# Table preload, operand splits and transposes around a seven-product SwiGLU

## The chip, the core and the metric

The kernel runs on one NeuronCore of a Trainium2 chip. The metric is the device time of one execution in microseconds, and the lower it is the better. A core has a matrix engine (PE, which loads a stationary operand of 128x128 and streams a moving one past it), a vector engine (DVE), a scalar engine (ACT, which evaluates functions from tables that have to be loaded), a general engine (POOL) and a queue engine (SP) from which most transfers are issued. Each engine takes its own instructions in order, and they wait for each other through semaphores. SBUF is the on-chip memory, PSUM the eight banks into which the PE accumulates.

## The reference

One residual encoder layer for a sequence of 512 tokens (with 16 learned tokens in front), model width D = 1024 and feed-forward width 2816:

```
xn = rmsnorm(h); proj = xn @ w_in          # both attentions' q, k, v
o_sb = stick-breaking attention            # 8 heads of 128
o_df = differential attention              # 8 heads, 2 maps each
gates = sigmoid(xn @ w_gate + b_gate)
h = h + (gates0 * (o_sb @ w_br_sb) + gates1 * (o_df @ w_br_df)) @ w_out
hn = rmsnorm(h)
h = h + (silu(hn @ w_ffn_gate) * (hn @ w_ffn_up)) @ w_ffn_down
out = rmsnorm(h)[16:]
```

All inputs are float32. The change touches the last three lines: the second norm, the SwiGLU and the final norm.

## The kernel before

**Precision.** Each float32 operand is split into a high part in the PE's fp32r type and a low part, the remainder: `split` has ACT copy the high part (L74, a CAST) and DVE subtract it (L75). A product is then three matmuls (`mm3`: L159 high x high, L160 and L161 high x low). Weights come as chunks of 512 KB, issued on SP's queue into `wst` (three buffers; `wsu`, two, for the up projection's), and are split to `wh` and `wl` (four buffers each).

**The stages that matter here.** The output projection (`accumulate(..., "out", ...)`) makes its left 512 columns in the four z accumulators and its right 512 in the four mm accumulators, and finishes the right half token tile by token tile: add to `hres` (L819), square with a running sum (L822), then `rstd`: Ln (L238) and Exp (L240) on ACT and a Newton step on DVE (L249, L245, L247), then the normed tile `hn` (L847). `turned(0)` and `turned(1)` transpose `hn` of tokens 0 to 255 and 256 to 511 on the PE into PSUM and take from it `hT_h` (ACT), `hT_l` (DVE) and a plain float32 copy `bf` (ACT, L863).

**The SwiGLU** runs over 22 column blocks f of 128 features. Block 0 is done plainly (`early`, in two token halves). The blocks 1 to 21 use a scheme that makes a 2x2 block product from seven products instead of eight: the token side is cut by token half and by half of the model width, and combined once into t1, t2, t3, t4 (`block_sums`, L868 to L876, each split into a high and a low part); the weight side of each block is combined into s2 and s1 (`c2`), s3 (`c3`) and s4 (`c4`). A block is `first` (a11 x b11 and a12 x b21, the weights of `c1`), `second` (s2 x t2, s1 x t1, s3 x t3) and `third` (a22 x t4, s4 x b22), 12 matmuls each. Between them ACT copies partial sums out of PSUM (qx, qy, L992 and L997), because the next product goes on in the same accumulator, and DVE adds them. The SiLU of the two token halves is L985 and L1009; the result is `aT`.

**The down projection** then streams `w_ffn_down` against splits of `aT` called `da` (eight buffers, made in `act`), left half in z, right half in mm, and ends tile by tile as above, with the final scaling on DVE (L1053) and ACT (L1055) and the stores on SP (L1054, L1056).

**What sets the order.** The tile framework's scheduler orders each engine's instructions from the program's order and priorities; evacuations of PSUM are lifted by `tc.high_priority`. `use_table` loads an ACT function set and keeps it in program order relative to other such pins, while ordinary activations may be placed on either side of it; where a function's set is not the loaded one, a load is put right ahead of it:

```
def use_table(name):
    tc.keep_in_program_order(nc.scalar.preload_act_table_set(name))
```

Buffers come from rings, so an instruction that writes one waits for the last reader of its former content.

Of the kernel before, what the change touches and what calls it, by code (L numbers as in the profile page):

```python
# [39 lines left out]
def block_kernel(ctx: ExitStack, tc: tile.TileContext, x, meta, norm_mix_g, w_in, w_gate, b_gate,  # L40
# [808 lines left out]
    def turned(tp_):  # L849
        cs = slice(tp_ * 256, (tp_ + 1) * 256)  # L850
        for k in range(0, KT, 2):
            pt = tr_tile()
            for i in range(2):
                for t in range(2):
                    nc.tensor.transpose(pt[:, (2 * i + t) * P:(2 * i + t + 1) * P],
                                        hn[:, 2 * tp_ + t, (k + i) * P:(k + i + 1) * P], ident)
            for i in range(2):
                g = g_ffn[:, k + i:k + i + 1]
                p = pt[:, i * 256:(i + 1) * 256]
                nc.scalar.activation(hT_h[:, k + i, cs], p, AF.Copy, scale=g)  # L860
                nc.vector.scalar_tensor_tensor(hT_l[:, k + i, cs], p, g, hT_h[:, k + i, cs].bitcast(F32),  # L861
                                               op0=ALU.mult, op1=ALU.subtract)
                nc.scalar.activation(bf[k // 4][tp_][:, (k + i) % 4], p, AF.Copy, scale=g)  # L863

    def block_sums():
        (b11, b12), (b21, b22) = bf
        sub, add = ALU.subtract, ALU.add
        nc.vector.tensor_tensor(b11, b11, b12, op=sub)  # L868
        nc.vector.tensor_tensor(b12, b22, b12, op=sub)
        nc.vector.tensor_tensor(b22, b11, b22, op=add)  # L870
        nc.vector.tensor_tensor(b21, b22, b21, op=sub)
        th, tl = tsum["t2"]
        nc.scalar.activation(th, b22, AF.Copy, scale=-1.0)
        nc.vector.scalar_tensor_tensor(tl, b22, -1.0, th.bitcast(F32), op0=ALU.mult, op1=sub)
        for n, v in (("t1", b11), ("t3", b12), ("t4", b21)):
            split(*tsum[n], v)  # L876
# [26 lines left out]


    with tc.tile_pool(name="ffn", bufs=1) as fp:
        aT = fp.tile([P, NFF, SEQ], F32, name="aT")
        gF = fp.tile([P, D], F32, name="gF")
        nc.gpsimd.dma_start(gF, norm_final_g.rearrange("(o d) -> o d", o=1).broadcast_to([P, D]))
        ffw_ctx = ExitStack()
        fw = ffw_ctx.enter_context(tc.tile_pool(name="ffw", bufs=1))  # L910
        fpools["w"] = fw
        ops = {}

        def chunk(n):
            return tuple(wpool.tile([P, KT, P], F32R, tag=t, name=t) for t in ("wh", "wl"))

        def c1(f):
            wh, wl = chunk(1)
            split(wh, wl, staged[at_of["fg", f]])
            ops[f, "a11"], ops[f, "a12"] = (wh[:, K1], wl[:, K1]), (wh[:, K2], wl[:, K2])  # L920

        def c2(f):
# [3 lines left out]
            nc.vector.tensor_tensor(s[:, K1], s[:, K2], g[:, K1], op=ALU.add)  # L926
            wh, wl = chunk(2)
            split(wh, wl, s)
# [3 lines left out]
        def c3(f):  # L932
            g, u = staged[at_of["fg", f]], staged[at_of["fu", f]]
            nc.vector.tensor_tensor(u[:, K1], g[:, K1], u[:, K1], op=ALU.add)
            wh, wl = chunk(3)
            split(wh, wl, u)
            ops[f, "s3"], ops[f, "a22"] = (wh[:, K1], wl[:, K1]), (wh[:, K2], wl[:, K2])

        def c4(f):
            g, s = staged[at_of["fg", f]], ops[f, "s"]  # L940
            nc.vector.tensor_tensor(g[:, K2], s[:, K1], g[:, K2], op=ALU.add)
            wh, wl = chunk(4)
# [22 lines left out]

        bank = {}

        def product(f, w, t, ps, start, stop):
            (wh, wl), (th, tl) = ops[f, w], tsum[t]
            mm3(ps, [(wh[:, k], wl[:, k], th[:, k], tl[:, k]) for k in range(4)], start, stop, True)  # L970

        def quarter(name, bufs=2):
            return fw.tile([P, 256], F32, tag=name, bufs=bufs, name=name)

        def first(f):
            e1, e2, e3 = mm_tile()[:, 0:256], mm_tile()[:, 0:256], z_tile()[:, 0, 0:256]
            sg = fw.tile([P, SEQ], F32, tag="sg", bufs=2, name="sg")
            bank[f] = e1, e2, e3, sg
            product(f, "a11", "b11", e1, True, True)
            product(f, "a12", "b21", e2, True, True)  # L980
            with tc.high_priority(offset=EVAC):
# [5 lines left out]
        def second(f):  # L987
            e1, e2, e3, sg = bank[f]
            qx, qy = quarter("qx"), quarter("qy")
            product(f, "s2", "t2", e1, False, True)  # L990
            with tc.high_priority(offset=EVAC):
                nc.scalar.copy(qx, e1)  # L992
            ready(at_job(c3, f) + 2)
            product(f, "s1", "t1", e3, True, True)
            product(f, "s3", "t3", e1, False, True)
            with tc.high_priority(offset=EVAC):
# [4 lines left out]
        def third(f, qx, qy):  # L1001
            e1, e2, e3, sg = bank[f]
            product(f, "a22", "t4", e1, False, True)
            with tc.high_priority(offset=EVAC):
                nc.vector.scalar_tensor_tensor(aT[:, f, T1], e1, -1.0, sg[:, T1], op0=ALU.mult, op1=ALU.mult)
            product(f, "s4", "b22", e3, False, True)
            with tc.high_priority(offset=EVAC):
# [22 lines left out]
        dw_ctx = ExitStack()  # L1030
        dw = dw_ctx.enter_context(tc.tile_pool(name="dw", bufs=1, reuse_waits="tile"))
        acts = []

        def act(half, k):
            m = half * NFF + k
            for i in range(len(acts), min(2 * NFF, m + 3)):
                a = dw.tile([P, 2, SEQ], F32R, tag="da", bufs=8, name="da")
                split(a[:, 0], a[:, 1], aT[:, i % NFF])
                acts.append(a)
            return acts[m][:, 0], acts[m][:, 1]  # L1040

# [57 lines left out]
```

## Time and profile before

| what | us |
|---|---|
| median of the runs (1008.54 to 1009.72, 3 runs) | 1009.62 |
| profiled execution, its own time | 1009.99 |
| its span, first to last instruction | 1008.2 |
| PE busy | 974.9 |
| PEld (weight loads, beside PE) | 880.4 |
| DVE busy | 659.9 |
| ACT busy | 544.7 |
| POOL busy | 109.7 |

The profile is one execution on the chip. Its page gives each engine's busy time, the groups of instructions by line with what ended the idle time ahead of them, and the chain that ended last; the trace behind it can be asked for waits, for windows of time, and for single instructions in order of time. In a row of an instruction stand its start, its duration, the engine, the line, the operation, output and input tile, and in brackets the idle time before it and what ended that. Matmuls are pipelined, so the distance between starts says more than a duration. The SwiGLU and the down projection take the span from 631.7 us to the end.

### The profile page before, as it was taken

The numbers are of one execution on the slowest core, as the hardware profiler recorded it, in microseconds if no ns is written. First come the engines' busy times: TensorE is split into PE (matmuls) and PEld (weight loads), VectorE is DVE, ScalarE is ACT, GpSimd is POOL, SyncE is SP. The second block draws the span as 40 slices with busy tenths as digits, with TensorE's granted clock in tenths as the row PEclk, the third lists the DMA queues.
The fourth block names the chain that finished last, engine by engine and source line by source line (L and its number), as shares of the span: only waits on it lengthen the run. The fifth ranks groups of instructions, "written<-read, shape, count | busy, mean of one in ns | idle before, by whom it ended". The sixth has DMA issues, their size and how long they took to land. (4 is left out here: it accounts for less than half of the span.)

```text
span 1008.2 us, 16022 instructions
## 1 busy us (share of the span) xinstructions
PE 974.9 (97%) x6285; PEld 880.4 (87%) x6285; DVE 659.9 (65%) x1214; ACT 544.7 (54%) x1026; POOL 109.7 (11%) x152
## 2 busy tenths in 40 slices
PE   7999999999999999999999999899999999899993
PEld 5999899998989999889878888899999999788883
DVE  7665446667777777777663335988888887645532
ACT  5655564555465666565643334764555555644436
POOL 4000000000022222122022320000000000000002
PEclk9999999999999999999999999999999999999997
DMA  6322222222333332333223252243333342322202
GB/s 197 105 64 63 84 85 63 85 64 71 93 90 87 104 99 72 83 85 96 74 83 105 93 178 64 63 128 104 112 99 115 95 118 71 123 87 105 88 17 84
DMA packets 129743, 93.13 MB, mean 92 GB/s; under 512 B 3682, under 2 KB 114435, under 8 KB 129667
## 3 DMA queue, kind: packets, MB, share of 16 engines
q1 hardware_dynamic: 127506, 85.09, 27.8%
q0 software_dynamic: 2000, 6.95, 2.7%
q8 instruction: 49, 0.80, 0.3%
q14 instruction: 28, 0.22, 0.1%
q10 hardware_dynamic: 160, 0.07, 0.0%
HBM read 85.67 MB, written 2.10 MB: 87 GB/s over the span
## 5 line engine op out<-in xcount | busy, mean ns | idle before, releaser
L75 DVE TENSOR_TENSOR wl<-wst,wh 128x1024 fp32r<-128x1024 f32 (+1 forms) x150 | 174.3, 1162 | 150.2 <-ACT wh L74 149.8
L159 PE MATMUL mm<-xT_h,wh 128*128 128x264 f32 (+2 forms) x776 | 249.9, 322 | 1.0 <-DVE dk L427 0.8
L160 PE MATMUL mm<-xT_l,wh 128*128 128x264 f32 (+2 forms) x776 | 247.2, 319 | 1.6 <-DVE xT_l L633 1.6
L161 PE MATMUL mm<-xT_h,wl 128*128 128x264 f32 (+2 forms) x776 | 246.8, 318 | 0.0
L74 ACT CAST wh<-wst 128x1024 fp32r<-128x1024 f32 (+1 forms) x150 | 148.6, 992 | 172.4 <-PE mm L160 112.0
L159 PEld LDWEIGHTS mm<-xT_h,wh 128*128 128x128 f32 x776 | 146.9, 189 | 11.3 <-PE tr L315 1.0
L160 PEld LDWEIGHTS mm<-xT_l,wh 128*128 128x128 f32 x776 | 146.8, 189 | 10.8 <-DVE xT_l L633 1.8
L161 PEld LDWEIGHTS mm<-xT_h,wl 128*128 128x128 f32 x776 | 146.7, 189 | 10.0
L159 PE MATMUL mm<-hT_h,wh 128*128 128x256 f32 x284 | 80.6, 286 | 1.8 <-ACT hT_h L860 0.9
L160 PE MATMUL mm<-hT_l,wh 128*128 128x256 f32 x284 | 81.1, 286 | 1.0 <-DVE hT_l L861 1.0
L161 PE MATMUL mm<-hT_h,wl 128*128 128x256 f32 x284 | 81.0, 286 | 0.2 <-DVE wl L75 0.2
L159 PEld LDWEIGHTS mm<-hT_h,wh 128*128 128x128 f32 x284 | 53.9, 191 | 2.7 <-ACT hT_h L860 1.4
L160 PEld LDWEIGHTS mm<-hT_l,wh 128*128 128x128 f32 x284 | 54.3, 191 | 1.5 <-DVE hT_l L861 1.4
L161 PEld LDWEIGHTS mm<-hT_h,wl 128*128 128x128 f32 x284 | 54.3, 191 | 0.4 <-DVE wl L75 0.4
L159 PE MATMUL mm<-o_h,wh 128*128 128x512 f32 x128 | 53.2, 415 | 0.0
L160 PE MATMUL mm<-o_l,wh 128*128 128x512 f32 x128 | 50.1, 391 | 0.8 <-DVE o_l L518 0.8
L161 PE MATMUL mm<-o_h,wl 128*128 128x512 f32 x128 | 50.1, 391 | 0.0
L159 PE MATMUL mm<-t_h,wh 128*128 128x256 f32 x168 | 47.4, 282 | 0.5 <-ACT qy L997 0.5
L160 PE MATMUL mm<-t_l,wh 128*128 128x256 f32 x168 | 47.2, 281 | 0.0
L161 PE MATMUL mm<-t_h,wl 128*128 128x256 f32 x168 | 47.2, 282 | 0.0
L159 PE MATMUL z<-wh,da 128*128 128x512 f32 (+1 forms) x110 | 41.3, 376 | 4.0 <-ACT da L74 4.0
L296 POOL COPY v_s<-vT 128x16 f32<-128x16 f32 x64 | 21.8, 369 | 210.0 <-ACT vT L301 210.0
(278 smaller groups left out, 2236.3 us busy)
## 6 DMA issues: line engine op xcount, KB each, us to landing
wst<-in_w_in_dram SPq DMA_DIRECT2D x46, 512.0 KB, 3.9
wst<-in_w_ffn_gate_dram SPq DMA_DIRECT2D x22, 512.0 KB, 3.8
wst<-in_w_ffn_down_dram SPq DMA_DIRECT2D x22, 512.0 KB, 3.5
wsu<-in_w_ffn_up_dram SPq DMA_DIRECT2D x21, 512.0 KB, 3.7
wst<-in_w_gate_dram SPq DMA_DIRECT2D x16, 512.0 KB, 4.1
dk<-dk POOLq DMA_DIRECT2D x16, 264.0 KB, 5.0
wst<-in_w_br_sb_dram SPq DMA_DIRECT2D x8, 512.0 KB, 3.5
wst<-in_w_br_df_dram SPq DMA_DIRECT2D x8, 512.0 KB, 3.5
```

The lines of the kernel that those rows point to most:

```text
L74: (hi_copy or nc.scalar.copy)(hi, src)
L75: (lo_eng or nc.vector).tensor_tensor(lo, src, hi.bitcast(F32), op=ALU.subtract)
L159: nc.tensor.matmul(ps, lhsT=ah, rhs=bh, start=(start and i == 0), stop=False, skip_group_check=skip)
L160: nc.tensor.matmul(ps, lhsT=ah, rhs=bl, start=False, stop=False, skip_group_check=skip)
L161: nc.tensor.matmul(ps, lhsT=al, rhs=bh, start=False, stop=(stop and i == n - 1), skip_group_check=skip)
L296: nc.gpsimd.tensor_copy(v_s[:, 32 * t:32 * t + NM], vT[:, (t + 1) * P:(t + 1) * P + NM])
```

## The change

Eight edits, all behind the output projection:

1. `turned` writes its transposes into z accumulators instead of the mm ring, and makes the `bf` copies in a loop of their own behind the hT parts.
2. `block_sums` splits t1 as soon as its sum is made, and t2 ahead of the sum for t4.
3. `c1(1)` and `first(1)` (the products of block 1) move ahead of the second token half of block 0; `first` keeps the matmuls, and the evacuation becomes `first_out`.
4. The job list therefore starts with `c1(2)`.
5. The first three splits of `aT` are made inside the last block, ahead of its `third` (`act_parts(3)`).
6. The eight `da` buffers are four in the SwiGLU's freed `wsu` and `s21` buffers and four in a new pool.
7. `use_table(LN_EXP)` moves from behind the block loop into the last block, right behind `third` with its last SiLU.
8. The pools of the SwiGLU stay open to the end.

```diff
     def turned(tp_):
         cs = slice(tp_ * 256, (tp_ + 1) * 256)
+        banks = [z_tile() for _ in range(2)]
         for k in range(0, KT, 2):
-            pt = tr_tile()
+            pt = banks[k // 4][:, k // 2 % 2]
...
-                nc.scalar.activation(bf[k // 4][tp_][:, (k + i) % 4], p, AF.Copy, scale=g)
+        for k in range(KT):
+            nc.scalar.activation(bf[k // 4][tp_][:, k % 4], banks[k // 4][:, k // 2 % 2, k % 2 * 256:(k % 2 + 1) * 256],
+                                 AF.Copy, scale=g_ffn[:, k:k + 1])
 
     def block_sums():
...
         nc.vector.tensor_tensor(b11, b11, b12, op=sub)
+        split(*tsum["t1"], b11)
         nc.vector.tensor_tensor(b12, b22, b12, op=sub)
         nc.vector.tensor_tensor(b22, b11, b22, op=add)
-        nc.vector.tensor_tensor(b21, b22, b21, op=sub)
         th, tl = tsum["t2"]
         nc.scalar.activation(th, b22, AF.Copy, scale=-1.0)
         nc.vector.scalar_tensor_tensor(tl, b22, -1.0, th.bitcast(F32), op0=ALU.mult, op1=sub)
-        for n, v in (("t1", b11), ("t3", b12), ("t4", b21)):
+        nc.vector.tensor_tensor(b21, b22, b21, op=sub)
+        for n, v in (("t3", b12), ("t4", b21)):
             split(*tsum[n], v)
...
+    def first(f):
+        bank[f] = [mm_tile()[:, 0:256], mm_tile()[:, 0:256]]
+        product(f, "a11", "b11", bank[f][0], True)
+        product(f, "a12", "b21", bank[f][1], True)
+
+    c1(1)
     turned(1)
+    first(1)
     for ps, key in zip(early, (("fg", 0), ("fu", 0))):
         proj(ps[:, 256:512], weights(key), hT, slice(256, 512))
     block_sums()
...
-        jobs = [(c1, 1), (c1, 2), (c2, 1), (c3, 1), (c4, 1)]
+        jobs = [(c1, 2), (c2, 1), (c3, 1), (c4, 1)]
...
+        dw, acts = None, []
+
+        def act_parts(upto):
+            for i in range(len(acts), min(2 * NFF, upto)):
+                pool, tag, bufs = ((dw, "da", 4), (fw, ("wsu", "s21")[i % 2], 2))[i % 8 < 4]
+                a = pool.tile([P, 2, SEQ], F32R, tag=tag, bufs=bufs, name="da")
+                split(a[:, 0], a[:, 1], aT[:, i % NFF])
+                acts.append(a)
...
         for f in range(1, NFF):
...
+            if f == NFF - 1:
+                act_parts(3)
             third(f, *rest)
+            if f == NFF - 1:
+                use_table(LN_EXP)
             ready(at_job(c4, f) + 2)
-        use_table(LN_EXP)
-        ffw_ctx.close()
         tp_ctx.close()
```

**Where instructions now stand.** On ACT at the end of the last token tiles (L822 squares, L238 Ln, L240 Exp, L1055 and L1071 the scaled output), before:

```order
L822 ACTIVATE sq,ssq<-hres 128x256
L1055 ACTIVATE outs<-outs,rs 128x512
L822 ACTIVATE sq,ssq<-hres 128x256
L238 ACT_TABLE_LOAD
L238 ACTIVATE rs<-ssq 128x1
L240 ACT_TABLE_LOAD
L240 ACTIVATE rs<-rs 128x1
L1055 ACTIVATE outs<-outs,rs 128x512
```

and now:

```order
L822 ACTIVATE sq,ssq<-hres 128x256
L1071 ACTIVATE outs<-outs,rs 128x512
L822 ACTIVATE sq,ssq<-hres 128x256
L238 ACTIVATE rs<-ssq 128x1
L240 ACTIVATE rs<-rs 128x1
L1071 ACTIVATE outs<-outs,rs 128x512
```

The two loads are gone from each of the four tiles, eight in all.

On ACT at the end of the last SwiGLU block (sg the SiLU, qx and qy the copies out of PSUM, wh the down projection's weights, da the splits of aT), before:

```order
L1009 ACTIVATE sg<-sg 128x256
L66 ACT_TABLE_LOAD
L992 COPY qx<-mm 128x256
L74 CAST wh<-wst 128x1024
L997 COPY qy<-mm 128x256
L74 CAST wh<-wst 128x1024 x2
L1009 ACT_TABLE_LOAD
L1009 ACTIVATE sg<-sg 128x256
L74 CAST da<-aT 128x512 x9
```

and now:

```order
L74 CAST da<-aT 128x512
L74 CAST wh<-wst 128x1024
L1018 ACTIVATE sg<-sg 128x256
L1001 COPY qx<-mm 128x256
L74 CAST wh<-wst 128x1024
L1006 COPY qy<-mm 128x256
L74 CAST wh<-wst 128x1024
L74 CAST da<-aT 128x512 x3
L74 CAST wh<-wst 128x1024
L1018 ACTIVATE sg<-sg 128x256
L66 ACT_TABLE_LOAD
L74 CAST da<-aT 128x512 x2
```

The table load stands behind the last SiLU, which has no load of its own now; the splits of aT stand ahead of it (three more stand further up, not shown), and qx stands right behind the SiLU of the block before. On the PE the first three matmuls of the down projection stand between s3 x t3 and a22 x t4 of the last block.

On DVE at the sums of the token side (bf the sums, t_l and hT_l the low parts of t1 to t4, wl those of weights), before:

```order
L869 TENSOR_TENSOR bf<-bf 128x1024
L75 TENSOR_TENSOR wl<-s_6817,wh 128x1024
L870 TENSOR_TENSOR bf<-bf 128x1024
L941 TENSOR_TENSOR wst<-s_6973,wst 128x512
L984 TENSOR_TENSOR sg<-mm,q_6852 128x256
L871 TENSOR_TENSOR bf<-bf 128x1024
L874 SCALAR_TENSOR_TENSOR t_l<-bf,t_h 128x1024
L75 TENSOR_TENSOR hT_l<-bf,hT_h 128x4x256
L75 TENSOR_TENSOR t_l<-bf,t_h 128x1024
L75 TENSOR_TENSOR wl<-wsu,wh 128x1024
```

and now:

```order
L871 TENSOR_TENSOR bf<-bf 128x1024
L958 TENSOR_TENSOR wst<-s_6969,wst 128x512
L873 TENSOR_TENSOR bf<-bf 128x1024
L993 TENSOR_TENSOR sg<-mm,q_6831 128x256
L75 TENSOR_TENSOR t_l<-bf,t_h 128x1024
L874 TENSOR_TENSOR bf<-bf 128x1024
L75 TENSOR_TENSOR hT_l<-bf,hT_h 128x4x256
L878 TENSOR_TENSOR bf<-bf 128x1024
L877 SCALAR_TENSOR_TENSOR t_l<-bf,t_h 128x1024
L75 TENSOR_TENSOR wl<-wsu,wh 128x1024
L75 TENSOR_TENSOR t_l<-bf,t_h 128x1024
```

The low part of t2 (L874, now L877) has fallen behind that of t3, and the weights' wl of block 1 has gone ahead of all sums. On the PE the 24 matmuls of `first(1)` stand around the last transposes, and the matmuls of `first(2)` behind the first one of s1 x t1. A little further on, DVE had the first sums of block 3 and of block 4 (L925) next to each other and block 3's second sum (L926) behind both; now block 4's first sum stands behind block 3's wl. The orders of SP and POOL are the same as before.

More of the change, by code (lines that the diff above doesn't have):

```diff
@@ L891, in block_kernel, with chunk, c1, product @@
         proj(ps[:, 0:256], weights(key), hT, slice(0, 256))
+    ops, bank = {}, {}
+    def chunk():
+        return tuple(wpool.tile([P, KT, P], F32R, tag=t, name=t) for t in ("wh", "wl"))
+    def c1(f):
+        wh, wl = chunk()
+        split(wh, wl, staged[at_of["fg", f]])
+        ops[f, "a11"], ops[f, "a12"] = (wh[:, K1], wl[:, K1]), (wh[:, K2], wl[:, K2])
+    def product(f, w, t, ps, start):
+        (wh, wl), (th, tl) = ops[f, w], tsum[t]
+        mm3(ps, [(wh[:, k], wl[:, k], th[:, k], tl[:, k]) for k in range(4)], start, True, True)
+    def first(f):
[3 more added lines that the diff above has]
+    c1(1)
     turned(1)
+    first(1)
     for ps, key in zip(early, (("fg", 0), ("fu", 0))):
@@ L908, in block_kernel @@
         nc.gpsimd.dma_start(gF, norm_final_g.rearrange("(o d) -> o d", o=1).broadcast_to([P, D]))
-        ffw_ctx = ExitStack()
-        fw = ffw_ctx.enter_context(tc.tile_pool(name="ffw", bufs=1))
+        inner = ExitStack()
+        fw = inner.enter_context(tc.tile_pool(name="ffw", bufs=1))
         fpools["w"] = fw
[L912 to L920, printed above, removed]
         def c2(f):
@@ L926, in c2 @@
             nc.vector.tensor_tensor(s[:, K1], s[:, K2], g[:, K1], op=ALU.add)
-            wh, wl = chunk(2)
+            wh, wl = chunk()
             split(wh, wl, s)
@@ L934, in c3 @@
             nc.vector.tensor_tensor(u[:, K1], g[:, K1], u[:, K1], op=ALU.add)
-            wh, wl = chunk(3)
+            wh, wl = chunk()
             split(wh, wl, u)
@@ L964, in at_job, with first_out @@
             return jobs.index((fn, f))
[L966 to L970, printed above, removed]
         def quarter(name, bufs=2):
             return fw.tile([P, 256], F32, tag=name, bufs=bufs, name=name)
-        def first(f):
-            e1, e2, e3 = mm_tile()[:, 0:256], mm_tile()[:, 0:256], z_tile()[:, 0, 0:256]
+        def first_out(f):
+            e1, e2 = bank[f]
             sg = fw.tile([P, SEQ], F32, tag="sg", bufs=2, name="sg")
-            bank[f] = e1, e2, e3, sg
-            product(f, "a11", "b11", e1, True, True)
-            product(f, "a12", "b21", e2, True, True)
+            bank[f] = e1, e2, z_tile()[:, 0, 0:256], sg
             with tc.high_priority(offset=EVAC):
@@ L989, in second @@
             qx, qy = quarter("qx"), quarter("qy")
-            product(f, "s2", "t2", e1, False, True)
+            product(f, "s2", "t2", e1, False)
             with tc.high_priority(offset=EVAC):
@@ L993, in second @@
             ready(at_job(c3, f) + 2)
-            product(f, "s1", "t1", e3, True, True)
-            product(f, "s3", "t3", e1, False, True)
+            product(f, "s1", "t1", e3, True)
+            product(f, "s3", "t3", e1, False)
             with tc.high_priority(offset=EVAC):
@@ L1002, in third @@
             e1, e2, e3, sg = bank[f]
-            product(f, "a22", "t4", e1, False, True)
+            product(f, "a22", "t4", e1, False)
             with tc.high_priority(offset=EVAC):
                 nc.vector.scalar_tensor_tensor(aT[:, f, T1], e1, -1.0, sg[:, T1], op0=ALU.mult, op1=ALU.mult)
-            product(f, "s4", "b22", e3, False, True)
+            product(f, "s4", "b22", e3, False)
             with tc.high_priority(offset=EVAC):
@@ L1014, in block_kernel, with act @@
         nc.vector.tensor_tensor(aT[:, 0], early[1], sg, op=ALU.mult)
-        ready(3)
-        first(1)
-        ready(4)
+        first_out(1)
+        ready(2)
         first(2)
+        first_out(2)
+        dw, acts = None, []
[5 more added lines that the diff above has]
+                acts.append(a)
+        def act(half, k):
+            act_parts(half * NFF + k + 3)
+            return acts[half * NFF + k][:, 0], acts[half * NFF + k][:, 1]
         for f in range(1, NFF):
@@ L1024, in block_kernel @@
                 first(f + 1)
+                first_out(f + 1)
+            if f == NFF - 1:
+                act_parts(3)
             third(f, *rest)
+            if f == NFF - 1:
+                use_table(LN_EXP)
             ready(at_job(c4, f) + 2)
-        use_table(LN_EXP)
-        ffw_ctx.close()
         tp_ctx.close()
[L1030 to L1040, printed above, removed]
+        dw = inner.enter_context(tc.tile_pool(name="dw", bufs=1, reuse_waits="tile"))
         def down_weights(key):
```

4 lines of the change are left out of this document (2 added, 2 removed).

## The prediction

> **What bounds the kernel now.** I read the page's busy times first, then the waits of the PE, then cut the span into windows around each wait, and last the timelines of ACT, DVE and PE in those windows.
>
> ```profile
> PE 974.9 (97%) x6285; PEld 880.4 (87%) x6285; DVE 659.9 (65%) x1214; ACT 544.7 (54%) x1026; POOL 109.7 (11%) x152
> PE z L159 <- ACT da L74: 4.0, 1, 4.0
> PE mm L160 <- DVE hT_l L861: 1.0, 2, 0.5
> PE mm L159 <- ACT hT_h L860: 0.9, 2, 0.7
> PE tr L855 <- DVE hn L847: 0.9, 1, 0.9
> 637.50:640.80 3.30, 1.76 (x12) 1.08 (x10) 2.83 (x8) 0.84 (x2) 0.00 (x0) 1.00 0.90 242
> 640.80:644.00 3.20, 3.10 (x14) 3.08 (x15) 3.20 (x8) 2.40 (x6) 0.00 (x0) 0.52 0.00 0
> 644.00:650.00 6.00, 4.83 (x37) 4.42 (x36) 5.40 (x9) 4.42 (x10) 0.00 (x0) 0.97 0.01 3
> 650.00:660.00 10.00, 9.79 (x83) 9.53 (x81) 9.88 (x11) 9.94 (x14) 0.56 (x1) 1.00 0.00 0
> 680.00:690.00 10.00, 8.03 (x65) 7.62 (x64) 8.28 (x15) 4.38 (x9) 0.00 (x0) 1.00 0.35 101
> 700.00:850.00 150.00, 150.00 (x1259) 150.00 (x1258) 126.25 (x196) 82.76 (x135) 0.00 (x0) 1.00 0.35 103
> 860.00:870.00 10.00, 5.41 (x41) 4.80 (x40) 5.51 (x9) 6.51 (x10) 0.00 (x0) 0.98 0.57 195
> 870.00:873.40 3.40, 3.40 (x9) 2.63 (x10) 3.40 (x6) 3.40 (x7) 0.00 (x0) 0.55 0.41 147
> 992.50:1008.20 15.70, 0.00 (x0) 0.00 (x0) 3.68 (x14) 9.31 (x16) 3.97 (x4) 0.61 0.27 101
> ```
>
> A row of the waits gives the total, how often, and the longest, in us. A window row gives its length, then busy time and count for PE, PEld, DVE, ACT, POOL, then the granted TensorE clock. The PE sets the pace: from 700 to 850 us it issues 1259 matmuls in 150 us, 0.119 us each, without a gap. In the part that the change touches it falls behind that pace in four places: 637.5 to 650 (entry of the SwiGLU), 680 to 690, 860 to 873.4 (entry of the down projection), and after 992.5, where it has nothing left and ACT is the busiest engine. The matmuls are the same before and after, so the change can win only what is lost there. I price three terms: A, the SwiGLU's entry up to 690; B, the down projection's entry; C, the tail.
>
> **C, the tail.** The rows of the last token tile, on PE, DVE and ACT, and two squares of earlier tiles (980.78 and 986.83):
>
> ```profile
> 992.21 0.28 PE L161 MATMUL z<-wh,da 128*128 128x256 f32 x1
> 998.35 0.41 DVE L819 TENSOR_TENSOR hres<-hres,z 128x256 f32<-128x256 f32 x1
> 980.78 0.63 ACT L822 ACTIVATE sq<-hres 128x512 f32<-128x512 f32 x1 [8.82 <-DVE hres L819]
> 986.83 0.64 ACT L822 ACTIVATE sq<-hres 128x512 f32<-128x512 f32 x1 [0.76 <-DVE hres L819]
> 999.38 1.28 ACT L238 ACT_TABLE_LOAD   x1
> 1000.68 0.30 ACT L238 ACTIVATE rs<-ssq 128x1 f32<-128x1 f32 x1
> 1000.99 1.28 ACT L240 ACT_TABLE_LOAD   x1
> 1002.29 0.20 ACT L240 ACTIVATE rs<-rs 128x1 f32<-128x1 f32 x1
> 1003.21 0.72 ACT L1055 ACTIVATE outs<-outs,rs 128x512 f32<-128x512 f32 x1 [0.72 <-issue]
> ```
>
> The last matmul ends at 992.49, but its sum L819 starts only at 998.35: the DVE is in order and stands behind the root of the tile before, whose Ln and Exp each carry a table load. With the loads one tile keeps ACT from 980.78 to 986.83, 6.0 us, while the PE takes 18 matmuls of 0.227 (from rows in the next part), 4.1 us; ACT falls behind by 2 us a tile. The changed order has no load between Ln and Exp anywhere in the tail: a tile then costs ACT 6.0 less two loads, 3.4 us, under the PE's 4.1. So L819 starts right after the last matmul, at about 992.56 instead of 998.35: 5.8 us. And in its own chain Ln starts at 999.38 instead of 1000.68, and Exp 0.32 later, at 999.70 instead of 1002.29: 2.6 us. **C is 5.8 + 2.6 = 8.4 us.** Bounds: 2.6, if something else keeps L819 late (a store that frees the last output buffer, say), and 8.4; I take 8.4, since that buffer's store belongs to a tile two steps earlier.
>
> The Trainium skill ("ScalarE: Activation LUTs", What ACT_TABLE_LOAD costs) puts a switch at about 2.66 us, 1.28 of load and 1.38 of drain. Here Ln starts 0.02 after its load ends, and no drain is seen; by the page the last chain would give back 5.3 instead of 2.6, and the time would be 2.7 us lower.
>
> **B, the down projection's entry.** ACT first, then PE:
>
> ```profile
> 858.92 1.28 ACT L66 ACT_TABLE_LOAD   x1
> 866.92 1.28 ACT L1009 ACT_TABLE_LOAD   x1
> 868.22 0.42 ACT L1009 ACTIVATE sg<-sg 128x256 f32<-128x256 f32 x1
> 869.18 4.26 ACT L74 CAST da<-aT 128x512 fp32r<-128x512 f32 x8 [0.55 <-DVE aT L1010]
> 860.64 0.39 PE L159 MATMUL mm<-hT_h,wh 128*128 128x256 f32 x1 [0.17 <-ACT qx L992]
> 862.78 0.38 PE L159 MATMUL mm<-t_h,wh 128*128 128x256 f32 x1 [0.46 <-ACT qy L997]
> 869.85 0.80 PE L159 MATMUL z<-wh,da 128*128 128x512 f32 x1 [3.96 <-ACT da L74]
> 873.26 0.40 PE L161 MATMUL z<-wh,da 128*128 128x512 f32 x1
> 875.08 0.39 PE L160 MATMUL z<-wl,da 128*128 128x512 f32 x1
> ```
>
> The LN_EXP load of L66 runs before the last SiLU, holds up the copy qx, and forces SiLU's set in again at 866.92; the first split of aT stands behind all that. The PE waits 0.17, 0.46 and 3.96; each wait also costs the 0.16 by which a last matmul's own 0.28 exceeds the pace of 0.119: 5.07. Then eight intervals take 3.41 (869.85 to 873.26) at a clock of 0.55; the next eight take 1.82 (to 875.08, 0.227 each): 1.59 more. **B is 6.7 us**, if all of it goes.
>
> In the changed order the splits of aT for blocks 0, 1 and 2 stand ahead of the last SiLU, and three matmuls of the down projection stand inside the last block. By the old clock, with qx in time, the PE is through s1 at 860.3, s3 at 861.7 (12 x 0.119), those three at 862.4, a22 at 863.9 and s4 at 865.3; six matmuls on the free bank last to 866.7. The other bank waits for the sum L1017, which DVE runs after s4 and one wl (cast from 863.8, a microsecond on ACT, 1.14 on DVE: 866.0), done at 866.4. So nothing is late. LN_EXP is then loaded once, near 868, and the first operand split behind that load is the eighth, which the PE needs six steps of 12 x 0.227 later. What hides the moved splits is DVE's slack: four of them, 0.6 us each, fall into the last two blocks, where DVE is busy 126.25 of 150 us. Without that cover they cost 2.4, so B's lower bound is 4.3.
>
> **A, the SwiGLU's entry.** The first products of block 1 now stand ahead of the second half of block 0, as filler for the waits on hn and hT.
>
> ```profile
> 638.75 0.87 PE L855 MATMUL tr<-ident,hn 128*128 128x128 f32 x6 [0.86 <-DVE hn L847]
> 640.37 0.87 DVE L861 SCALAR_TENSOR_TENSOR hT_l<-tr,pcol,hT_h 128x256 fp32r<-128x256 f32 x2
> 654.17 1.22 DVE L871 TENSOR_TENSOR bf<-bf 128x1024 f32<-128x1024 f32 x1
> 655.31 1.22 DVE L874 SCALAR_TENSOR_TENSOR t_l<-bf,t_h 128x1024 fp32r<-128x1024 f32 x1
> 670.68 0.69 DVE L925 TENSOR_TENSOR s<-wsu 128x512 f32<-128x512 f32 x1 [2.68 <-DMA wsu<-in_w_ffn_up_dram]
> 671.29 0.68 DVE L926 TENSOR_TENSOR s<-s,wst 128x512 f32<-128x512 f32 x1
> 664.99 0.28 PE L159 MATMUL mm<-t_h,wh 128*128 128x256 f32 x1
> DMA to landing us min/median/max: 3.7/3.8/6.5
> ```
>
> Old loss from 637.5 to 650: 12.5 us less 63 matmuls of 0.119, 5.0. But the DVE was full here too (9.88 of 10 from 650 to 660), and its work does not shrink. After hn, which comes when it came before, it has up to the low part of t2: eight 128x1024 operations of 1.14 (start to start), eight 128x512 of 0.61, eight hT_l of 0.4 and one sum of 0.35: 9.1 + 4.9 + 3.2 + 0.35 = 17.6 from 638.7, so t2 comes at 656.3, no earlier than its 656.5 in this trace. The PE, freed of its old waits, would get there at 637.5 + 16 transposes of 0.13 + 109 matmuls of 0.119 = 652.6. It waits some 3.5 us there, in several pieces. Next it needs wh of block 2, which ACT casts behind t4's high part (done near 656.1) and a table load: 656.1 + 1.28 + 1.0 = 658.4, another 1.0; then the copies qx and qy, 0.8. Block 1 ends at about 663.7, against 664.99 in the row: with an allowance of one matmul of block 2, a gain of 1.2. Further on, DVE stood 2.68 us before block 4's first sum with block 3's second sum behind it; the new order pairs each block's sums. That stall starved the PE in 680 to 690: 65 matmuls for 84, 2.4 us. So A can reach 1.2 + 2.4 = 3.6. Against it, some 2.5 of 3.3 us idle around 656 may halve the clock, as 1.54 of 3.3 did before 640.8 (0.52 in the next window); on 12 matmuls that costs 1.1. I take **A = 3.0**, between 2.5 and 3.6; its bounds are 0 (all given back to the DVE) and 7.4 (5.0 + 2.4).
>
> The Trainium skill ("TensorE: Matmul & The Clock Gate", What's actually happening) has the clock fall after an idle window of about 3.4 us. The trace has it fall after a window in which the PE was busy 1.76 of 3.30. By the page A would be 3.6, by the row 2.5.
>
> Edits at no cost: the transposes go to the z banks, which the first half of the out projection has left. Their new wait, for the eight bf copies of the first token pair, ends before Ln of the last tile, which stands behind these copies on ACT, and the transposes need that tile's hn anyway; late, it costs the 0.9 of that wait again. The orders of SP and POOL stay.
>
> **Sum.** 3.0 + 6.7 + 8.4 = 18.1. The profiled execution took 1009.99 (1.8 around its span of 1008.2); less 18.1 is **991.9 us**. The median of the runs, 1009.62, lies 0.4 lower, inside the uncertainty.
>
> **Rivals.** First, the SwiGLU's entry becomes a loss: the DVE's pace takes all of A and the clock halves for two windows more, 2 us in all: 1009.99 - 15.1 + 2 = 996.9. For it speaks the full DVE and ACT (9.94 of 10); against it, that most of the new waits are slack in which a slow clock is free.
> Second, the tail keeps its loads, so that the change does not do what it says there: 991.9 + 8.4 = 1000.3. Against it stands the built order.
> Third, the moved splits crowd DVE and B gives only 4.3: 994.3.
> Fourth, slower: the two buffers for w_ffn_up set the pace of every block. A wl frees one, the load lands, and two sums, a wl, a sum of qy, a third sum, the sum of sg and the next wl follow: 0.6 + 0.6 + 1.14 + 0.34 + 0.6 + 0.34 + 1.14 = 4.8, with 3.8 to land 8.6, under the PE's 84 x 0.119 = 10.0. It decides from a landing of 5.2 on, and eats 18.1 over 20 blocks at 6.1; with the longest, 6.5, the time is 1009.99 - 18.1 + 20 x 1.3 = 1017.9. The median landing speaks against it.
>
> **How the numbers follow.** Forecast 0.70, loss at the entry 0.13, third 0.09, tail loads 0.04, slower 0.02, and 0.02 for A at its upper bound (987.5). The forecast's own range, A from 1 to 5, is 989.9 to 993.9; with most of the third and part of the first rival, and some of A's upper bound, 988.3 to 996. Faster and slower count from 0.2%, 2 us, about what this kernel's runs can tell: faster 0.97, same 0.01, slower 0.02.
>
> **What would show it.** C: no table loads on L238 and L240, and about 7.3 us from the last matmul's end to the end of the span instead of 15.7. B: no PE wait for da above 0.5 us, and a clock of 1.00 through that entry. A: about 4 us of PE waits on t1, t2 or wh between 648 and 659, and a full 680 to 690. Wrong would be a tail above 9 us, a new wait in the steady blocks, or a block 1 that ends after 665.

## The result, and the profile after

The changed kernel takes 992.94 us (median of 4 runs, 992.87 to 993.24); the kernel before took 1009.67 beside it. The ratio is 0.9837, with a 95% interval from 0.982 to 0.9854. The prediction was 991.9, in a range from 988.3 to 996.0. The profiled execution took 992.9, with a span of 991.1, against 1009.99 and 1008.2 before: 17.1 us less, where the three terms promised 18.1.

The busy times of the page, the three longest waits of PE from 600 us on, and windows like those shown of before:

```profile
PE 970.6 (98%) x6285; PEld 877.1 (88%) x6285; DVE 662.0 (67%) x1214; ACT 534.0 (54%) x1017; POOL 110.0 (11%) x152
PE mm L160 <- DVE t_l L877: 1.1, 1, 1.1
PE mm L159 <- ACT wh L74: 1.0, 1, 1.0
PE mm L160 <- DVE hT_l L862: 0.7, 2, 0.4
637.50:640.80 3.30, 3.21 (x28) 3.01 (x27) 2.62 (x5) 1.33 (x4) 0.00 (x0) 1.00 0.76 209
640.80:644.00 3.20, 2.98 (x24) 2.68 (x24) 3.20 (x6) 2.60 (x5) 0.00 (x0) 1.00 0.00 0
644.00:650.00 6.00, 4.93 (x38) 4.32 (x36) 5.96 (x11) 4.88 (x12) 0.00 (x0) 1.00 0.00 0
650.00:660.00 10.00, 7.35 (x55) 6.74 (x56) 10.00 (x12) 9.96 (x13) 0.54 (x1) 1.00 0.11 30
680.00:690.00 10.00, 10.00 (x86) 10.00 (x85) 8.62 (x14) 5.52 (x9) 0.00 (x0) 1.00 0.37 106
700.00:850.00 150.00, 150.00 (x1259) 150.00 (x1258) 126.67 (x196) 83.94 (x138) 0.00 (x0) 1.00 0.35 103
860.00:870.00 10.00, 10.00 (x55) 8.54 (x54) 7.96 (x13) 7.88 (x11) 0.00 (x0) 1.00 0.48 164
982.90:991.10 8.20, 0.00 (x1) 0.00 (x0) 2.60 (x8) 1.73 (x5) 1.74 (x3) 0.62 0.34 129
```

The windows 680 to 690 and 860 to 870 are full. No wait for da is left. The steady stretch from 700 to 850 is what it was, 1259 matmuls in 150 us. The tail is 8.2 us instead of 15.7. But the wait at the SwiGLU's entry has not gone. From 637.5 to 650 PE is busy 11.1 of 12.5, against 9.7 before; but from 650 to 660 it is busy 7.35 of 10, against 9.79, while DVE is full and ACT nearly so. Most of the wait has moved there.

To say what each stage gave, I count from one matmul that both kernels have: the first of block 0's first token half. Behind it I take the first matmul of s4 in blocks 1, 4 and 20. Of before and then of the changed kernel, in the timeline of PE:

```profile
631.72 0.28 PE L159 MATMUL mm<-hT_h,wh 128*128 128x256 f32 x1
663.56 0.28 PE L159 MATMUL z<-hT_h,wh 128*128 128x256 f32 x1
695.65 0.28 PE L159 MATMUL z<-hT_h,wh 128*128 128x256 f32 x1
856.01 0.28 PE L159 MATMUL z<-hT_h,wh 128*128 128x256 f32 x1
```

```profile
631.20 0.28 PE L159 MATMUL mm<-hT_h,wh 128*128 128x256 f32 x1
663.15 0.28 PE L159 MATMUL z<-hT_h,wh 128*128 128x256 f32 x1
692.68 0.28 PE L159 MATMUL z<-hT_h,wh 128*128 128x256 f32 x1
853.11 0.28 PE L159 MATMUL z<-hT_h,wh 128*128 128x256 f32 x1
982.62 0.28 PE L161 MATMUL z<-wh,da 128*128 128x256 f32 x1
```

The start itself is 0.5 earlier; executions of one program differ by as much there (630.98 to 631.66 in three of the changed kernel). Block 1 then stands at 31.84 before and 31.95 after, block 4 at 63.93 and 61.48, block 20 at 224.29 and 221.91, and the last matmul's end (992.49, and 982.62 + 0.28) at 360.77 and 351.70. So **A is 2.4, B 6.7 (9.1 less 2.4), C 7.5**, and with the 0.5 of the start 17.1. Nothing of A lies before block 1; all of it lies between blocks 1 and 4.

One execution in all, of the run e7_tr_ring below, took 2462.44 us; the record does not show why, and it is left out of that run's median.

### The profile page after: what moved, and what is told of

Read it like the earlier page. It is cut to its first block, busy times and chain, and to the rows that moved or that the text cites. A ratio compares the mean times of both kernels' runs of the same rounds, so it can differ in the third digit from the quotient of the medians.

```text
span 991.1 us, 16004 instructions
## 1 busy us (share of the span) xinstructions
PE 970.6 (98%) x6285; PEld 877.1 (88%) x6285; DVE 662.0 (67%) x1214; ACT 534.0 (54%) x1017; POOL 110.0 (11%) x152
## 4 chain that ended last, share of the span: by engine, by line
PE 90%; DVE 4%; ACT 3%; DMA 1%; issue 1%; POOL 0%; SPq 0%; DVEq 0%; ACTq 0%; POOLq 0%
PE mm L159 22%; PE mm L160 21%; PE mm L161 21%; PE z L159 6%; PE z L160 6%; PE z L161 6%; PE tr L315 2%; PE z L446 1%; PE z L447 1%; ACT wh L74 1%; PE tr L290 1%; PE z L339 0%; PE tr L327 0%; ACT bf L865 0%; DMA xs<-in_x_dram 0%
## 5 line engine op out<-in xcount | busy, mean ns | idle before, releaser
L474 ACT ACTIVATE pr<-pr,nm 128x144 f32<-128x144 f32 (+3 forms) x64 | 36.3, 569 | 14.2 <-DVE nm L472 14.1
```

The lines of the kernel that those rows point to most:

```text
L474: nc.scalar.activation(pr[:, c], pr[:, c], AF.Exp, bias=nm[:, c:c + 1], accum_out=ls[:, t, c:c + 1])
```

## Experiments

Positions in the table are counted in this way. The tail is the time from the last matmul's end to the end of the span. The runs are told by name below.

| run | median us | block 1 | block 4 | block 20 | last matmul | tail |
|---|---|---|---|---|---|---|
| before (profile) | 1009.67 | 31.84 | 63.93 | 224.29 | 360.77 | 15.7 |
| changed kernel | 992.94 | 31.95 | 61.48 | 221.91 | 351.70 | 8.2 |
| e1_pin_only | 1002.34 | 31.43 | 63.77 | 224.14 | 360.02 | 8.0 |
| e2_no_pin | 1000.63 | 32.14 | 61.67 | 222.10 | 352.09 | 15.4 |
| e3_old_da | 1000.76 | 33.56 | 63.12 | 223.55 | 359.16 | 8.2 |
| e4_left_early | 992.26 | 32.00 | 61.53 | 221.96 | 351.74 | 7.4 |
| e5_old_sums | 994.70 | 31.28 | 62.82 | 223.19 | 352.96 | 8.2 |
| e6_first_back | 993.19 | 32.20 | 61.76 | 222.19 | 351.96 | 8.2 |
| e7_tr_ring | 994.44 | 32.76 | 62.24 | 222.67 | 352.44 | 8.1 |
| e9_no_silu_pin | 993.26 | 32.01 | 61.54 | 221.97 | 351.74 | 8.3 |
| e11_both | 992.25 | 32.07 | 61.64 | 222.07 | 351.86 | 7.4 |

Medians of different runs carry the start's chance of half a microsecond and more, so verdicts below a microsecond rest on the positions.

### The pin alone (e1_pin_only)

On the kernel before:

```
             third(f, *rest)
+            if f == NFF - 1:
+                use_table(LN_EXP)
             ready(at_job(c4, f) + 2)
-        use_table(LN_EXP)
```

> The kernel before with one edit: LN_EXP is loaded behind the last SiLU. Theory (the terms B and C are separate, and the pin carries all of C but only a part of B): C gives the 7.5 us that the changed kernel's profile shows (tail 15.7 to 8.2). At the down projection's entry the two loads ahead of the last SiLU go (0.17 + 0.46 of waits, 1.28 of load), but the first split of aT still stands behind that SiLU and now behind one load of 1.28, so it starts about 1.6 us earlier and the PE still waits some 3 us for da, with the slow clock behind it. Time 1009.7 - 9.1 = 1000.6, between 999.5 and 1001.5. Rival (the loads alone caused the entry's stall, and the early splits add nothing): 1009.7 - 7.5 - 6.7 = 995.5, no wait for da above 0.5.

Measured: 1002.34 (6 runs, 1000.03 to 1003.36), a ratio to before of 0.9927, interval 0.9914 to 0.994. The median lies 0.8 above the theory's range. The tail is 8.0, so the pin carries all of C, 7.7 here. But the entry of the down projection gains only 0.6 (135.88 from block 20 to the last matmul, against 136.48). ACT's timeline there, and PE's wait and clock:

```profile
865.69 0.42 ACT L1009 ACTIVATE sg<-sg 128x256 f32<-128x256 f32 x1 [0.20 <-DVE sg L1008]
866.12 1.28 ACT L66 ACT_TABLE_LOAD   x1
867.41 4.26 ACT L74 CAST da<-aT 128x512 fp32r<-128x512 f32 x8
PE z L159 <- ACT da L74: 3.6, 1, 3.6
868.00:872.00 4.00, 3.92 (x10) 3.09 (x11) 3.94 (x7) 3.68 (x8) 0.00 (x0) 0.57 0.52 159
```

The SiLU comes early, but the load that the pin put behind it now stands between it and the first split of aT. PE waits 3.6 instead of 4.0, and the clock falls all the same. The rival, that the loads alone made the stall, is out: it needed no wait for da. The 1.6 us that the theory gave the pin at this place was too much as well: it gave 0.6.

### All but the pin (e2_no_pin)

On the changed kernel, the edit above undone.

> The changed kernel with one edit undone: LN_EXP is again loaded wherever the scheduler puts it, which is ahead of the copy qx of the last block, so that SiLU's set comes back behind it and Ln and Exp carry their own loads in the tail. Theory: the tail is 15.7 us again (plus 7.5), and the entry loses only the 0.5 to 1.0 us by which one load delays qx, since the splits of aT stand ahead of the last SiLU: 992.9 + 7.5 + 0.8 = 1001.2, between 1000.2 and 1002. Rival (the entry's gain hangs on the pin too): the PE waits 3 us or more for da and the clock falls, 992.9 + 7.5 + 5 = 1005.4 or above.

Measured: 1000.63 (4 runs, 1000.55 to 1001.05), as the theory had it, and 7.7 over the changed kernel. The tail is 15.4. At the entry, ACT and its two loads:

```profile
856.29 1.28 ACT L66 ACT_TABLE_LOAD   x1
862.73 1.66 ACT L74 CAST da<-aT 128x512 fp32r<-128x512 f32 x3
865.35 1.28 ACT L1018 ACT_TABLE_LOAD   x1
```

Both loads are back, and PE does not wait for da at all: the splits stand ahead of the second load. The entry takes 129.99, against 129.79 in the changed kernel and 136.48 before. So B is the work of the early splits, 6.5 of 6.7 without any help from the pin, and C is the work of the pin.

### The buffers of da as before (e3_old_da)

```
-                pool, tag, bufs = ((dw, "da", 4), (fw, ("wsu", "s21")[i % 2], 2))[i % 8 < 4]
-                a = pool.tile([P, 2, SEQ], F32R, tag=tag, bufs=bufs, name="da")
+                a = dw.tile([P, 2, SEQ], F32R, tag="da", bufs=8, name="da")
...
-            if f == NFF - 1:
-                act_parts(3)
...
+        inner.close()
         tp_ctx.close()
```

> The changed kernel with the buffers of da as before (eight buffers in a pool that opens when the SwiGLU's pools are closed), so that no split of aT can stand ahead of the last SiLU; the pin and the entry edits stay. Theory: B loses what the pin alone does not give, 6.7 - 1.6 = 5.1: 998.0, between 996.8 and 999; the PE waits about 3 us for da, at a lower clock behind it. Rival (the early splits are worth nothing once the pin is there): 992.9.

Measured: 1000.76 (4 runs, 999.48 to 1000.95), 1.8 us over the theory's range. From block 20 to the last matmul it takes 135.61, which is 5.8 more than the changed kernel: the theory's 5.1 within a microsecond, with a wait for da of 3.6. The other part of the miss is in a place that the edit does not touch. Windows of this run, and of the changed kernel:

```profile
656.00:660.00 4.00, 1.93 (x12) 1.73 (x13) 4.00 (x5) 3.97 (x6) 0.04 (x1) 0.95 0.11 25
660.00:664.00 4.00, 3.66 (x19) 3.46 (x19) 2.38 (x5) 1.48 (x3) 0.56 (x1) 0.63 0.82 245
```

```profile
656.00:660.00 4.00, 2.43 (x18) 2.23 (x19) 4.00 (x6) 3.97 (x5) 0.54 (x1) 1.00 0.26 75
660.00:664.00 4.00, 3.65 (x31) 3.45 (x31) 3.69 (x7) 1.79 (x4) 0.06 (x1) 1.00 0.79 256
```

The same instructions and the same waits, but here the granted clock falls behind them, 19 matmuls run in the time of 31, and block 1 is 1.6 later. Only one execution of this run has a profile. Two of its others took as long (1000.85 and 1000.95) and one took 999.48, so how often the clock falls in this program is not known.

What the edit takes away is the buffers, not the call. When the changed kernel is built with `act_parts(3)` alone left out, every engine's order of instructions is the same, since `da` tiles in the SwiGLU's own buffers let the scheduler move the splits up by itself. So of edits 5 and 6 it is the buffers of edit 6 that matter.

### POOL's left products out of the tail (e4_left_early)

```
-                outs.append(dw.tile([P, D], F32, tag="outs", name="outs", bufs=2))
-                nc.gpsimd.tensor_tensor(outs[t][:, 0:512], hres[:, t, 0:512], gF[:, 0:512], op=ALU.mult)
+        def left(t):
+            lefts.append(dw.tile([P, 512], F32, tag="lefts", name="lefts", bufs=4))
+            nc.gpsimd.tensor_tensor(lefts[t], hres[:, t, 0:512], gF[:, 0:512], op=ALU.mult)
...
-        accumulate(dw, "down", act, NFF, 0, 0, lambda t: None, "z")
+        accumulate(dw, "down", act, NFF, 0, 0, left, "z")
```

> The changed kernel with POOL's products of the left 512 columns with the final gain made right behind the down projection's first half, in four buffers of their own, instead of in the tail; the work is the same. In the changed kernel's tail DVE operations that start beside POOL's products run long: a 128x1 L249 1.33 us instead of 0.22, the 128x512 scaling L1069 1.60 instead of 0.49, L826 0.67 instead of 0.2; so the last L819 starts at 983.86 although its matmul ended at 982.90. Theory (the two engines get in each other's way in SBUF): with the left products gone, L249 of tile 1 takes 0.22, L1069 of the tile before the last 0.5 to 0.9, the last L819 starts within 0.2 of the last matmul's end, and the tail is 7.3 us instead of 8.2: 992.0. Rival (the long DVE rows have another cause, such as the store of the output buffer): rows and tail as they are, 992.9.

Measured: 992.26 (4 runs, 991.55 to 992.58). The tail of the changed kernel first, then that of this run (DVE and POOL):

```profile
975.32 1.29 POOL L1080 TENSOR_TENSOR outs<-hres,gF 128x512 f32<-128x512 f32 x1 [2.79 <-DVE hres L819]
976.03 0.21 DVE L239 TENSOR_SCALAR rs<-ssq 128x1 f32<-128x1 f32 x1 [0.79 <-ACT sq L822]
976.59 1.33 DVE L249 SCALAR_TENSOR_TENSOR rs<-rs 128x1 f32<-128x1 f32 x1 [0.35 <-ACT rs L240]
976.62 1.29 POOL L1079 TENSOR_TENSOR outs<-hres,gF 128x512 f32<-128x512 f32 x1
981.74 1.60 DVE L1069 TENSOR_SCALAR outs<-outs,rs 128x512 f32<-128x512 f32 x1
981.77 1.29 POOL L1079 TENSOR_TENSOR outs<-hres,gF 128x512 f32<-128x512 f32 x1 [0.91 <-DMA out_dram<-outs]
983.02 0.90 POOL L1080 TENSOR_TENSOR outs<-hres,gF 128x256 f32<-128x256 f32 x1
983.26 0.67 DVE L826 SCALAR_TENSOR_TENSOR ssq<-ssq 128x1 f32<-128x1 f32 x1
983.86 0.41 DVE L819 TENSOR_TENSOR hres<-hres,z 128x256 f32<-128x256 f32 x1
```

```profile
976.71 0.22 DVE L249 SCALAR_TENSOR_TENSOR rs<-rs 128x1 f32<-128x1 f32 x1 [0.35 <-ACT rs L240]
981.47 0.74 POOL L1083 TENSOR_TENSOR rights<-hres,gF 128x256 f32<-128x256 f32 x1 [0.61 <-DVE rs L245]
981.71 0.79 DVE L1069 TENSOR_SCALAR lefts<-lefts,rs 128x512 f32<-128x512 f32 x1
982.42 0.15 DVE L826 SCALAR_TENSOR_TENSOR ssq<-ssq 128x1 f32<-128x1 f32 x1
982.74 0.28 PE L161 MATMUL z<-wh,da 128*128 128x256 f32 x1
983.06 0.42 DVE L819 TENSOR_TENSOR hres<-hres,z 128x256 f32<-128x256 f32 x1 [0.49 <-PE z L161]
```

In the changed kernel three DVE operations overlap a product of POOL, end with it or just behind it, and take 1.33, 1.60 and 0.67. Two of them take 0.22 and 0.15 once the product is elsewhere, and the third takes 0.79, because one short product still runs beside it. The last L819 now waits for PE and nothing else, and the tail is 7.4, which is the prediction's 7.3. Rows and tail moved as the theory has it, and the rival, that they stay, does not hold.

The edit takes away two things at once, though. The product at 981.77 had itself stood 0.91 for the store of an output buffer, and with buffers of its own it no longer does. That the product beside it makes a DVE row long is shown by L249 and L826, which write no output buffer. How much of the 0.8 came from the late start of that product is not shown.

### The order of the sums (e5_old_sums)

```
         nc.vector.tensor_tensor(b11, b11, b12, op=sub)
-        split(*tsum["t1"], b11)
         nc.vector.tensor_tensor(b12, b22, b12, op=sub)
         nc.vector.tensor_tensor(b22, b11, b22, op=add)
+        nc.vector.tensor_tensor(b21, b22, b21, op=sub)
...
-        nc.vector.tensor_tensor(b21, b22, b21, op=sub)
-        for n, v in (("t3", b12), ("t4", b21)):
+        for n, v in (("t1", b11), ("t3", b12), ("t4", b21)):
```

> The changed kernel with the sums and splits of t1 to t4 written in the order of before; everything else as changed. Positions are counted from the first matmul of block 0's first token half, to take out what comes earlier: s4 of block 1 starts 31.95 us behind it in the changed kernel (31.84 before), s4 of block 4 61.48 behind it (63.93 before). So all of A lies between blocks 1 and 4. In the built order of this run DVE has the first sum of block 4 ahead of the second sum of block 3 again, as before, where it stood 2.68 us for a load of w_ffn_up. Theory (A is that stall and nothing else, and the order of the sums decides it): s4 of block 4 is back at 63.5 to 64.2, the time 992.9 + 2.4 = 995.3. Rival (A is the filler matmuls and the banks at the entry): block 4 stays at 61.5, 992.9, or lower, since t2 comes one DVE operation earlier.

Measured: 994.70 (4 runs, 993.85 to 995.28). DVE's first sum of block 4 in this run, and in the changed kernel, there with block 4's second sum behind it:

```profile
669.81 0.69 DVE L941 TENSOR_TENSOR s<-wsu 128x512 f32<-128x512 f32 x1 [2.45 <-DMA wsu<-in_w_ffn_up_dram]
```

```profile
670.40 0.68 DVE L942 TENSOR_TENSOR s<-wsu 128x512 f32<-128x512 f32 x1
671.11 0.69 DVE L943 TENSOR_TENSOR s<-s,wst 128x512 f32<-128x512 f32 x1
```

In the changed kernel DVE does not wait for this load. The stall of before (2.68, in the row at 670.68 quoted in the prediction) is back as 2.45, and blocks 1 to 4 take 31.54, against 29.53 in the changed kernel and 32.09 before. So the order of the sums of t decides whether DVE stands for block 4's load: 2.0 us. But block 1 is 0.7 earlier than in the changed kernel. On DVE the low part of t2 no longer stands behind that of t3, and it is done 24.3 behind the first matmul of block 0 instead of 25.4. So block 4 stands at 62.82, short of the theory's 63.5. Theory and rival each had a part; net the changed order wins 1.3.

### The filler (e6_first_back)

```
     turned(1)
-    first(1)
...
+        first(1)
         first_out(1)
```

> The changed kernel with block 1's first products behind both halves of block 0 again, as before, so that the PE has no filler for its waits on hn and hT_l; the paired order of the sums of blocks 3 and 4 stays in the built order. Theory (the DVE's work up to the low part of t2 sets block 1's end, and filler that moves no DVE work gives nothing there): block 1's s4 starts 31.6 to 32.4 us behind the first matmul of block 0, block 4's 61.2 to 62, the time 992.4 to 993.4; the waits move from t1, t2 and wh to hT. Rival (the filler is worth the waits that it fills, 0.9 on hn and 1.9 on hT before): 992.9 + 2 = 994.9 or more.

Measured: 993.19 (4 runs, 992.60 to 994.65), and 0.3 later at every position from block 1 on. The positions are the theory's: the filler moved the waits and gave almost nothing. Its reason holds only in part, since DVE's work did move: the low part of t2 is done at 26.4 instead of 25.4, and block 1 is still only 0.3 later. The clock fell here too (0.59 in the mean from 648 to 652). Behind that PE still waits 0.8 for t2, so most or all of the fall may have been free, but no run shows it.

### The banks of the transposes (e7_tr_ring)

`turned` as before: `pt = tr_tile()`, and each `bf` copy behind its `hT_l`.

> The changed kernel with the transposes in the mm ring again and the bf copies behind each pair, as before. Theory (these are edits at no cost, since DVE's chain sets the entry): block 1's s4 31.6 to 32.6 us behind the first matmul of block 0, the time 992.9 within 0.7. Rival (the ring makes the transposes wait for PSUM that is still being read, up to the 0.9 us that the PE waited on hT_h before, and once more behind it): 994 to 994.7.

Measured: 994.44 (median of 3, 993.66 to 994.61). Block 1 is 0.8 later and all behind it 0.75. PE's waits for hn and hT are about those of before:

```profile
PE mm L160 <- DVE hT_l L861: 1.3, 2, 0.7
PE mm L159 <- ACT hT_h L860: 0.9, 2, 0.7
PE tr L855 <- DVE hn L847: 0.9, 1, 0.9
```

This is the rival's side: the edit that I had at no cost is worth 0.75. The later waits have shrunk in this run, to 0.3 for t2 and 0.3 for the weights of block 2 (1.1 and 1.0 in the changed kernel), and the low part of t2 is done at 24.0 instead of 25.4. So it is not DVE's work up to t2 that sets the entry here. The run undoes the banks and the separate loop of the bf copies together; which of the two counts is not shown.

### Without the second load of SiLU's set (e9_no_silu_pin)

```
     block_sums()
-    use_table("silu_and_others")
```

> The changed kernel without the pinned load of SiLU's set behind the sums. In its profile ACT loads a table twice there: at 649.96, put ahead of block 0's SiLU, and at 656.74, the pin, with only SiLUs, copies and casts between. Theory (the pin is a second load of the same set, and the wait of 1.0 us for wh of block 2 stands behind it): one load fewer, that wait shrinks to 0.3 or less, block 1's s4 31.0 us behind the first matmul of block 0, 991.9. Rival (DVE, full in this stretch, has the next operand late anyway): block 1 within 0.3 of 31.95 and 992.6 to 993.

Measured: 993.26 (4 runs, 992.80 to 993.73), no position moved by more than 0.1. The load is gone and wh of block 2 comes 1.3 earlier, but PE now waits 0.8 for the next thing:

```profile
656.76 1.05 ACT L74 CAST wh<-s 128x1024 fp32r<-128x1024 f32 x1
658.25 1.05 ACT L74 CAST wh<-wsu 128x1024 fp32r<-128x1024 f32 x1 [0.43 <-PE mm L160]
659.20 0.37 ACT L1000 COPY qx<-mm 128x256 f32<-128x256 f32 x1
659.62 0.39 PE L159 MATMUL mm<-hT_h,wh 128*128 128x256 f32 x1 [0.82 <-ACT qx L1000]
```

The rival had the position right, the time within 0.3, and the engine wrong: it is not DVE that is late next, it is ACT's copy qx, which this run's order puts behind a cast that itself waits 0.43 for PE.

### The changed kernel again (e10_again, e10_again2), and both gains (e11_both)

> The changed kernel again, nothing edited, for its profile alone. In four profiles with the same instructions in the SwiGLU's entry (the changed kernel and three of the other runs) the clock stayed at 1.00 from 656 to 664 in three and fell to 0.50 in one, where block 1 came 1.6 us later; the waits were the same. Theory (whether the clock falls depends on how the waits lie to something outside the program): block 1's s4 starts either 31.9 to 32.2 us behind block 0's first matmul with the clock at 1.00, or 33.3 to 33.7 with a window at 0.5, and nothing between. Rival (the program of that one run made it fall): 31.9 to 32.2 in every profile of this kernel.

> The same kernel a third time, the same two possibilities: 31.9 to 32.2 at a clock of 1.00, or 33.3 to 33.7 with a window at 0.5.

The two executions took 992.80 and 993.45. Block 1 stood at 32.02 and 31.97, at a clock of 1.00 both times. With the runs above, that is one fall of the clock in six profiles of this stretch, so the rival is not ruled out by these two alone. What speaks against it is the old entry. In the two profiles with its instructions the clock from 641 to 645 was 0.58 in the mean in the kernel before, and 1.00 from 640 to 650 in e1_pin_only, where block 1 came 0.4 earlier.

> The two edits that take something away from the changed kernel's critical stretches: POOL's left products made early, and no second load of SiLU's set. Theory (from the runs of each alone: the tail gives 0.8, the load nothing, since the copy qx then stands behind another cast): block 1's s4 at 32.0, a tail of 7.4, 992.2. Rival (the two free time for each other): below 991.5.

Measured: 992.25 (5 runs, 991.89 to 992.89), with a tail of 7.4 and block 1 at 32.07: the sum of the two runs alone, no more. The version with the left products early is 0.7 below the changed kernel by the medians (992.26 against 992.94) and 0.8 by the tail.

## Why the prediction was right, and where it was off

The three terms came to 16.6 of the 18.1 that were forecast. The profiled execution came out 17.1 faster because its SwiGLU also started 0.5 earlier; executions of one program differ by as much there, so that half microsecond is luck.

**B, 6.7 predicted, 6.7 measured.** No wait for da is left, the clock is 1.00 through the entry, and the four moved splits did not crowd DVE: from 840 to 863, where they stand, it is busy 17.59 of 23, and PE has no wait at all. What the prediction left open is which edit does it. e1_pin_only and e2_no_pin say: the early splits, almost alone.

**C, 8.4 predicted, 7.5 measured.** The mechanism held, though the 6.0 us a tile that the prediction gave ACT hold two waits of some 0.7 for DVE, so that the chain through both engines, not ACT alone, was slower than PE. There are no loads at L238 and L240 now, and from the start of the last L819 to the end of the span it takes 7.24 us (991.1 less 983.86) instead of 9.85 (1008.2 less 998.35), the 2.6 of the working. The term that was mis-sized is the 5.8 for the start of L819, "right after the last matmul, at about 992.56". It started 0.96 behind the last matmul's end, because DVE, which the prediction took to be free once ACT was fast, was held by its own long operations beside POOL's products. With the products gone (e4_left_early) the term is what was forecast. The prediction had set aside a store that frees the last output buffer, as belonging to a tile two steps earlier; POOL's product at 981.77 did wait 0.91 for one.

**A, 3.0 predicted, 2.4 measured, with one step wrong.** The stall at block 4 was priced at 2.4 (its 19 missing matmuls of 0.119 make 2.3), and the stretch from block 1 to block 4 gave 2.6. The step that failed is "a gain of 1.2" at the end of block 1. It gave nothing (31.84 to 31.95). Two rows of DVE in the changed kernel, block 1's first sum and the low part of t2, show where the count went wrong:

```profile
638.84 0.69 DVE L942 TENSOR_TENSOR s<-wsu 128x512 f32<-128x512 f32 x1 [0.65 <-DMA wsu<-in_w_ffn_up_dram]
655.33 1.22 DVE L877 SCALAR_TENSOR_TENSOR t_l<-bf,t_h 128x1024 fp32r<-128x1024 f32 x1
```

The prediction let DVE run 17.6 without a pause from hn to t2. It took 18.4 (hn is done at 638.19, t2 at 656.55), and 0.65 of that is the wait for a load of w_ffn_up, which the count left out although 0.3 of it stood in the trace of before. Counted from block 0, t2 was due at 24.6 and came at 25.4; wh of block 2 was due at 26.7 (658.4 in the times of before) and let PE go on at 27.9 (659.13 in the new trace). That is 1.2 late, the whole gain. The new order of t1 to t4 was counted but not set against the old one; by e5_old_sums it costs block 1 0.7. One of the prediction's signs of being wrong did show: in the times of before, block 1 ends at 665.1, just after 665. Its waits of PE on t1, t2 or wh came to 2.5, not about 4. The allowance of 0.6 for a halved clock was not needed in the profiled execution. It was needed in one of six, and then cost 1.6, not the 1.1 of the working.

Undone one at a time, the order of the sums costs 1.3, the banks 0.75 and the filler 0.3 at block 20, together 2.3 of A's 2.4. Single edits undone need not add up like this, and each of these runs also shifts the order of other instructions. The prediction gave the banks nothing, as an edit at no cost; they are worth 0.75 of A, and the filler, which it took for the source of the 1.2, is worth 0.3.

**Rivals.** The entry did become a wait (7.35 of 10 busy from 650 to 660), but not a loss over all of A, as the first rival had it. No loads are left in the tail, DVE was not crowded, and w_ffn_up's buffers set no pace: the steady blocks are full.

## What to carry to other kernels

When a load or a wait is taken out of an engine's order, look at what the in-order engine has to run next and beside whom: here three of the gains were cut by the next thing in the same queue or by a neighbour (the pinned load ahead of the first split, the copy qx behind a cast, DVE's scaling beside POOL). At the down projection's entry, splits that can move ahead of the stage's end because their buffers are free were worth 6.5, and shortening the chain in front of them by a table load only 0.6. And an order of small sums that looks local can decide, some blocks later, whether an engine stands in front of a load.

## What the runs showed of the hardware

**DVE beside POOL.** A 128x1 DVE operation with two inputs in SBUF took 1.33 us when POOL's product started 0.03 behind it, and 0.22 without; the scaling of 128x512 took 1.60 against 0.49. A 128x1 TENSOR_SCALAR (L239 at 976.03), which reads one tensor, a constant and a column of ssq, took its usual 0.21 while POOL's product at 975.32 was running. The Trainium skill ("SBUF — State Buffer", Who interferes with whom) says that the two engines share a pair of ports, that a DVE instruction with two SBUF inputs or in a 2-port mode, which tensor_scalar can enter, contends with POOL, that one with at most one input does not, and that the loser blocks for the whole instruction. These rows agree that the pair is contended and that a DVE row then ends with POOL's product or behind it. They do not tell who wins: in e4_left_early L247, a 128x1 TENSOR_TENSOR with two inputs in SBUF, also started 0.03 ahead of a product (981.44 and 981.47) and took its usual 0.16.

**The clock.** The same instructions with the same waits were followed by a fall of the granted clock in one execution and not in another (0.95 and then 0.63 against 1.00 in the windows quoted with e3_old_da; PE busy 1.93 of 4 there). PE busy 1.99 of 4 in the same window of e10_again2 was followed by no fall, nor was 1.85 of 3.30 from 637.5 to 640.8 in e1_pin_only. So my reading, that 1.76 busy of 3.30 brings the fall, is no rule. The Trainium skill ("TensorE: Matmul & The Clock Gate", What's actually happening) says that activity is judged over windows of about 3.4 us that run freely and do not start with the kernel. That would make the fall a matter of where the waits lie in them, which fits; no run here shows the windows themselves, and whether e3_old_da's fall was chance stays open.
